# A five-engine schedule of a decoder layer: QK in pairs of banks, a store tile, another down-projection order, new durations and priorities

## The chip, the cores and the metric

One Trainium2 chip, all 8 cores, each with two of the 16 sequences; the cores share no data. The metric is the device time of the slowest core in microseconds (us). These kernels have a second, slower state: the cores of one die (four cores) show a lower granted TensorE clock and the run takes longer (in one run of the changed kernel 0.84 of full speed and 4912.6 us, in a fast one 0.99 and 4295.3 us).

## The reference

One layer of a decoder, d = 1024, sequence 4096, 8 heads of 64, FFN width 2816, with a final norm:

```python
xn = rms_norm(h, mix_norm);  z = xn @ w_in                  # 1024 x 3080
y_conv = gate_b * causal_depthwise_conv(gate_c * u, conv_w)    # 512 wide, 3 taps
# forgetting attention: logit[t, s] = q_t.k_s / 8 + c[t] - c[s], causal, c = cumsum(log f)
y_attn = softmax(logits) @ v                                   # 8 heads x 64
h = h + group_rms_norm(concat(y_conv, y_attn)) @ w_o
gu = rms_norm(h) @ w_gate_up;  h = h + (silu(g) * up) @ w_down   # 2816 wide
h = h + sigmoid(rms_norm(h) @ w_ple_gate + b) * (p @ w_ple_proj)
return rms_norm(h, final_norm)
```

## The kernel before

The kernel works in 16 blocks of 512 tokens a core. It doesn't issue instructions in the order of its source. Each operation is put on record with an engine, a reckoned duration and a priority (`key`; one block is 1.0 wide, smaller is earlier). A scheduler plays the program through on the host, picks on each engine the ready operation with the smallest key, and emits that static order with semaphores. Reckoned durations and keys therefore change only the order and which buffer a tile gets, never the work. On the chip an engine waits at its next instruction: in the trace of the kernel before, VectorE runs nothing from 2314.2 us until an addition that waits for a fetch of h starts at 2321.1.

```python
LAT = {"pe": 0.26, "act": 0.13, "dve": 0.12, "pool": 0.2, "sp": 0.1}
DMA_RATE = 300e3
# ... in Prog.schedule:
                c = clock[e]
                cand = None
                early = None
                for o in lst:
                    r = tile_ready(o)
                    if r is None:
                        continue
                    if r <= c:
                        if cand is None or (o.key, o.seq) < (cand.key, cand.seq):
                            cand = o
                    elif early is None or (r, o.key, o.seq) < early[:3]:
                        early = (r, o.key, o.seq, o)
                if cand is not None:
                    st = (c, cand)
                elif early is not None:
                    st = (early[0], early[3])
                else:
                    continue
                if best is None or st[0] < best[0]:
                    best = st
# ...
            o.start = st
            o.end = st + o.dur
            clock[e] = o.end
```

Attention: each group of four key tiles gets four PSUM banks, four row-tiled QK products (64 of 128 rows, two at once, 4 ns from start to start in the trace; on the diagonal four more for the decay), four exponentials on ScalarE, four PV products. `av` follows `LOOK` units behind.

```python
        LOOK = 4
        # ...
                if ui % 4 == 0:
                    quad = [Tile(qS) for _ in range(4)]

                    def fqk(e, quad=quad, kt=kt, dg=dg, h=h):
                        for dec in ((False, True) if dg else (False,)):
                            for i in range(4):
                                r = slice(64 * (i % 2), 64 * (i % 2) + 64)
                                k_ = ((kt + i) // 2) * 128
                                cc = 128 * i if dg else 0
                                ins = e.matmul(quad[i].ap()[:, cc:T],
                                               lhsT=sel[r, h * 128:(h + 1) * 128] if dec else KT[r, h, k_:k_ + 128],
                                               rhs=crow[r, cc:T] if dec else QT[r, h, cc:T],
                                               start=not dec, stop=dec or not dg)
                        return ins
                    rd = [BKT[h][kt // 4], BQT[h]]
                    if dg:
                        rd += [Bcrow, B["sel"]]
                    last_qk = P.op("pe", fqk, (3 * MM if dg else 2 * MM) + 0.2, K(i), reads=rd, writes=quad,
                                   after=[last_qk])
                st = quad[ui % 4]
                P.op("act", lambda e, st=st, pt=pt, c0=c0, kt=kt, h=h: e.activation(
                    out=pt.ap()[:, c0:T], in_=st.ap()[:, c0:T], func=AF.Exp, bias=bK[:, kt, h:h + 1], scale=1.0),
                    0.17 + (T - c0) / 1200.0, K(i), reads=[st, BbK], writes=[pt])
```

The down projection of each FFN half, the final norm, and the priorities of the main loop (`n` is the block of output projection, FFN, PLE and final norm; PLE is the per-layer embedding, the reference's line with `p`; attention works one block ahead, QKV two):

```python
            for dh in range(2):
                k = L()
                wd = [(wload(g, k), nn) for g, nn in dn[dh]]
                for tt in range(4):
                    k = L()
                    t = Tile(qD)
                    mats = []
                    j = 0
                    for wt, nn in wd:
                        for i in range(nn):
                            mats.append((actT[:, j, tt * 128:(tt + 1) * 128],
                                         (lambda wt=wt, i=i: wt.ap()[:, i * 512:(i + 1) * 512]), [BactT[j], wt]))
                            j += 1
                    mm_group(t, mats, k, [])
                    add_to_h(t, tt, dh, k, scale=0.5)
# ... finish(n, key):
            P.op("dve", lambda e, h=h, c=c: e.scalar_tensor_tensor(out=h[:], in0=h[:], scalar=stat[:, c:c + 1],
                                                                   in1=gfin[:], op0=ALU.mult, op1=ALU.mult),
                 1.25, key, reads=[Bstat[c], B["gfin"]], writes=[Bh[tt]])
            r0 = blk * T + tt * 128
            P.dma("pool", lambda e, h=h, r0=r0: e.dma_start(out=y_d[sq, r0:r0 + 128, :], in_=h[:]), key, f"h{tt}",
                  128 * 4096, reads=[Bh[tt]])
# ... the main loop, b = float(n):
                load_h(n, b - 0.15)
            wo(n, b + 0.0, b + 0.05)
                # ...
                conv(n + 1, b + 0.08, b + 0.5)
                attention(n + 1, b + 0.05, b + 0.8)
            # ...
            ffn(n, b + 0.07, b + 0.68)
            # ...
            ple(n, b + 0.70, b + 0.80)
            finish(n, b + 0.80)
                # ...
                qkv(n + 2, b + 0.5, b + 0.685, b + 0.8, b + 1.055)
```

## Time and profile before

| | before |
|---|---|
| median of the first 4 runs (lowest to highest) | 4422.84 us (4420.14 to 4934.05; the highest is a slow-state run) |
| profiled run: span of the slowest core, its mean granted clock | 4421.6 us, 0.979 |
| TensorE, VectorE, ScalarE busy | 95%, 61%, 53% |

TensorE's busy share is of little use here, since records of successive matmuls overlap (for 512 columns a record lasts 381 ns, the starts lie 216 ns apart). The prediction shows the lines of the profile and splits the span by the distance between the starts of successive matmuls instead (a slot for fewer than 512 columns is taken in proportion: starts lie 163, 109 and 56 ns apart for 384, 256 and 128 columns; what is left over is a mode change, a half-clock slot or a wait).

### The profile page before, as it was taken

How to read it: one execution, taken by the hardware profiler on the slowest of the kernel's cores; microseconds unless marked ns; L12 is line 12 of the kernel's file. 1: busy time of each engine (PE TensorE's matmuls, PEld its weight loads, DVE VectorE, ACT ScalarE, POOL GpSimd, SP SyncE). 2: the span in 40 equal slices, each digit the busy share in tenths (PEclk: the TensorE clock that was granted, in tenths of full speed). 3: DMA queues.
4: the chain of work that ended last, by engine and by line, in shares of the span. 5: the costliest groups of instructions: out<-in, count | busy, mean ns of one | idle time of the engine just before them, and what ended most of it. 6: DMA issues, size and time to landing. Idle time of an engine off the chain costs nothing.

```text
span 4421.6 us, 74502 instructions; the slowest of 8 cores (4402.8 to 4421.6 us)
## 1 busy us (share of the span) xinstructions
PE 4189.6 (95%) x23472; PEld 2006.0 (45%) x23472; DVE 2709.3 (61%) x5508; ACT 2356.9 (53%) x4417; POOL 355.1 (8%) x915
## 2 busy tenths in 40 slices
PE   6898999999999999999989999999999999999987
PEld 3444454454544445444454444545444454444434
DVE  6666676575655656546676766757566565564534
ACT  3333454555656667667234444545566566666721
POOL 2110000000000000001000000000000000000000
PEclk9898999999999999999999999999999999999998
DMA  8796434343433433324444353434334343333232
GB/s 192 168 225 196 134 123 150 129 158 110 139 118 112 160 103 128 116 95 127 143 142 140 117 176 127 155 121 143 119 115 163 109 136 111 106 132 99 93 112 98
DMA packets 172779, 590.32 MB, mean 134 GB/s; under 512 B 19696, under 2 KB 28272, under 8 KB 172400
## 3 DMA queue, kind: packets, MB, share of 16 engines
q1 hardware_dynamic: 127952, 453.80, 30.7%
q0 software_dynamic: 44448, 131.76, 11.8%
q8 instruction: 202, 3.31, 0.3%
q14 instruction: 177, 1.45, 0.1%
HBM read 556.80 MB, written 61.87 MB: 140 GB/s over the span
## 4 chain that ended last, share of the span: by engine, by line
PE 87%; DVE 4%; issue 3%; DMA 3%; ACT 3%; POOL 0%; DVEq 0%; another core or an unknown queue 0%; ACTq 0%; POOLq 0%; SPq 0%
PE ps L577 58%; PE ps L833 11%; PE ps L880 7%; PE ps L1084 5%; PE ps L623 2%; PE ps L701 2%; ACT P L891 1%; DMA xs<-x 1%; DMA y<-h 1%; PE ps L1079 1%; PE ps L863 1%; DMA h<-x 1%; DVE xnTd L628 0%; PE ps L845 0%; DMA wslot<-wscr 0%
## 5 line engine op out<-in xcount | busy, mean ns | idle before, releaser
L891 ACT ACTIVATE P<-ps,bK 128x512 bf16<-128x512 f32 (+3 forms) x2304 | 1364.9, 650 | 747.6 <-PE ps L880 469.4
L577 PE MATMUL ps<-xnTd,wslot 128*128 128x512 bf16 x5792 | 1344.8, 381 | 21.7 <-DVE actT L1030 6.1
L577 PEld LDWEIGHTS ps<-xnTd,wslot 128*128 128x128 bf16 x5792 | 557.4, 98 | 699.4 <-issue 87.8
L833 PE MATMUL ps<-P,VA 128*65 128x512 bf16 (+3 forms) x2304 | 661.3, 368 | 36.5 <-DVE yTa L852 12.7
L577 PE MATMUL ps<-wslot,actT 128*128 128x512 bf16 x2816 | 661.8, 379 | 0.6 <-DVE h L981 0.2
L577 PE MATMUL ps<-xnTq,wslot 128*128 128x512 bf16 x2400 | 571.2, 381 | 8.6 <-DMA wslot<-wscr 4.3
L1026 DVE SCALAR_TENSOR_TENSOR tb<-th,ps 128x512 bf16<-128x512 f32 x352 | 241.2, 685 | 401.1 <-ACT th L1023 382.9
L577 PEld LDWEIGHTS ps<-wslot,actT 128*128 128x128 bf16 x2816 | 271.5, 98 | 322.5 <-issue 19.3
L1023 ACT ACTIVATE th<-ps 128x512 f32<-128x512 f32 x352 | 210.5, 598 | 387.4 <-PE ps L577 385.6
L833 PEld LDWEIGHTS ps<-P,VA 128*65 128x65 bf16 x2304 | 243.5, 111 | 373.1 <-issue 219.1
L981 DVE SCALAR_TENSOR_TENSOR h<-ps,h 128x512 f32<-128x512 f32 x256 | 176.2, 689 | 344.9 <-PE ps L577 323.0
L577 PEld LDWEIGHTS ps<-xnTq,wslot 128*128 128x128 bf16 x2400 | 230.0, 98 | 281.6 <-issue 37.3
L880 PE MATMUL ps<-QT,KT 64*128 64x512 bf16 (+3 forms) x2304 | 338.4, 367 | 12.5 <-ACT P L891 11.7
L895 POOL TENSOR_SCALAR_AFFINE_SELECT P<-P 128x128 bf16<-128x128 bf16 x512 | 180.5, 363 | 1764.8 <-ACT P L891 1674.2
L1030 DVE TENSOR_TENSOR actT<-tb,ps 128x512 bf16<-128x512 bf16 x352 | 240.9, 684 | 121.8 <-PE ps L577 111.3
L607 ACT ACTIVATE xnbf<-h 128x1024 bf16<-128x1024 f32 x196 | 206.3, 1053 | 178.6 <-DVE h L978 88.8
L1084 PE MATMUL ps<-wslot,xnTd 128*128 128x256 bf16 x2048 | 252.3, 278 | 0.0
L1084 PEld LDWEIGHTS ps<-wslot,xnTd 128*128 128x128 bf16 x2048 | 203.8, 100 | 50.8 <-issue 1.6
L909 DVE TENSOR_TENSOR rs<-rs,ps 128x512 f32<-128x512 f32 (+1 forms) x192 | 130.2, 679 | 111.5 <-ACT rs L907 109.3
L623 PE MATMUL ps<-identb,xnbf 128*128 128x128 bf16 x1536 | 125.5, 229 | 62.6 <-DVE xnbf L614 17.7
L628 DVE TENSOR_TENSOR xnTd<-ps,gpc_s 128x1024 bf16<-128x1024 bf16 x132 | 159.0, 1219 | 24.6 <-PE ps L623 23.6
L880 PEld LDWEIGHTS ps<-QT,KT 64*128 64x128 bf16 x2304 | 66.5, 94 | 229.7 <-issue 225.8
(123 smaller groups left out, 4098.0 us busy)
## 6 DMA issues: line engine op xcount, KB each, us to landing
wslot<-wscr SPq DMA_DIRECT2D x795, 512.0 KB, 3.8
h<-x POOLq DMA_DIRECT2D x64, 512.0 KB, 6.0
y<-h POOLq DMA_DIRECT2D x64, 512.0 KB, 7.1
xs<-x POOLq DMA_DIRECT2D x60, 512.0 KB, 4.5
wslot<-wpack POOLq DMA_DIRECT2D x53, 512.0 KB, 14.1
wscr<-wslot SPq DMA_DIRECT2D x53, 512.0 KB, 10.5
wslot<-wscr SPq DMA_DIRECT2D x30, 256.0 KB, 2.8
pbf<-p POOLq DMA_DIRECT2D x16, 256.0 KB, 5.4
```

The costliest lines, as they stand in the source:

```text
L577: ins = e.matmul(out, lhsT=l, rhs=r, start=(i0 + i == 0), stop=(i0 + i == n - 1))
L607: P.op("act", lambda e: e.activation(out=xb.ap()[:], in_=src(), func=AF.Square, accum_out=stat[:, col:col + 1]), 1.25, key - 0.1, reads=[B ...
L623: ins = e.transpose(out=pv[:, kc * 128:(kc + 1) * 128], in_=xb.ap()[:, kc * 128:(kc + 1) * 128], identity=identb[:])
L833: P.op("pe", lambda e, o=o, kt=kt, h=h, pt=pt, c0=c0, first=first, last=last, ui=ui, dg=dg: e.matmul(o.ap()[0:65, c0:T], lhsT=VA[:, kt, h, ...
L880: ins = e.matmul(quad[i].ap()[:, cc:T], lhsT=sel[r, h * 128:(h + 1) * 128] if dec else KT[r, h, k_:k_ + 128], rhs=crow[r, cc:T] if dec els ...
L891: P.op("act", lambda e, st=st, pt=pt, c0=c0, kt=kt, h=h: e.activation(out=pt.ap()[:, c0:T], in_=st.ap()[:, c0:T], func=AF.Exp, bias=bK[:, ...
L895: P.op("pool", lambda e, pt=pt, c0=c0: e.affine_select(out=pt.ap()[:, c0:c0 + 128], in_=pt.ap()[:, c0:c0 + 128], pattern=[[1, 128]], compa ...
L981: P.op("dve", lambda e: e.scalar_tensor_tensor(out=hs, in0=t.ap()[:], scalar=scale, in1=hs, op0=ALU.mult, op1=ALU.add), 0.72, key - 0.05, ...
L1023: P.op("act", lambda e, tg=tg, th=th: e.activation(out=th.ap()[:], in_=tg.ap()[:], func=AF.Tanh, scale=0.5), 0.6, k - 0.1, reads=[tg], wri ...
L1026: P.op("dve", lambda e, tg=tg, th=th, tb=tb: e.scalar_tensor_tensor(out=tb.ap()[:], in0=th.ap()[:], scalar=1.0, in1=tg.ap()[:], op0=ALU.ad ...
L1030: P.op("dve", lambda e, tu=tu, tb=tb, j=j: e.tensor_tensor(out=actT[:, j, :], in0=tb.ap()[:], in1=tu.ap()[:], op=ALU.mult), 0.69, k - 0.1, ...
L1084: ins = e.matmul(tg.ap()[:, i * 256:(i + 1) * 256], lhsT=xnT[1][:, kc, ts], rhs=w8(wg[i])[:, kc, 0:256], start=False, stop=(kc == 7 and i ...
```

## The change

Its intent: a schedule that reckons nearer to the trace (in the trace of before successive 512-column VectorE and ScalarE instructions start 600 and 570 ns apart, though each lasts some 685 ns, on VectorE mostly where the second does not read the first's result, some 790 ns or more where it does; a change between row-tiled and full matmuls costs 96 ns there and 91 ns back), a finer unit for QK, a final norm that frees h at once, an FFN that finishes token tile by token tile, and new priorities. No arithmetic and no byte is added or removed.

```diff
--- before.py
+++ after.py
@@ -60,10 +60,13 @@
 
 class Op:
-                 "npred", "succ", "tag", "lab", "ready", "seq", "start", "end", "vis", "pos", "snap", "waits", "extra")
-
-
-LAT = {"pe": 0.26, "act": 0.13, "dve": 0.12, "pool": 0.2, "sp": 0.1}
+                 "npred", "succ", "tag", "row", "lab", "ready", "seq", "start", "end", "vis", "pos", "snap", "waits", "extra")
+
+
+LAT = {"pe": 0.26, "act": 0.10, "dve": 0.10, "pool": 0.15, "sp": 0.1}
+SELF = {"pe": 0.0, "act": 0.05, "dve": 0.07, "pool": 0.05, "sp": 0.0}
+HEAD = {"pe": 0.0, "act": 0.115, "dve": 0.09, "pool": 0.04, "sp": 0.0}
+SWITCH = 0.1
 DMA_RATE = 300e3
 
 
@@ -170,15 +175,23 @@
                 c = clock[e]
                 cand = None
                 early = None
+                rows = []
                 for o in lst:
                     r = tile_ready(o)
                     if r is None:
                         continue
-                    if r <= c:
+                    if r <= c and o.row:
+                        rows.append(o)
+                    elif r <= c:
                         if cand is None or (o.key, o.seq) < (cand.key, cand.seq):
                             cand = o
                     elif early is None or (r, o.key, o.seq) < early[:3]:
                         early = (r, o.key, o.seq, o)
+                if rows:
+                    o = min(rows, key=lambda o: (o.key, o.seq))
+                    full = sum(1 for f in o.alloc[0].pool.free if f[0] <= c) >= 4
+                    if row_mode or cand is None or (full and (o.key, o.seq) < (cand.key, cand.seq)):
+                        cand = o
                 if cand is not None:
                     st = (c, cand)
                 elif early is not None:
@@ -207,9 +220,12 @@
                 t.pool.free.remove(f)
                 t.idx = f[1]
                 o.extra.extend(f[2])
+            if e == "pe" and o.row != row_mode:
+                st += SWITCH
+                row_mode = o.row
             o.start = st
             o.end = st + o.dur
-            clock[e] = o.end
+            clock[e] = o.end - min(HEAD[e], 0.5 * o.dur)
             if o.sem is not None:
                 t0 = max(o.end + 1.4, dma_free[0])
                 dma_free[0] = t0 + o.nbytes / DMA_RATE
@@ -232,7 +248,7 @@
                     r = 0.0
                     for d in s.deps:
                         if d.eng == s.eng and d.sem is None:
-                            v = d.end if s.eng == "pe" else d.end + 0.065
+                            v = d.end + SELF[s.eng]
                         else:
                             v = d.vis
                         if v > r:
@@ -805,7 +821,7 @@
     def attention(m, k0, k1):
         sq, blk = divmod(m, nblk)
         decay(m, k0 - 0.02)
-        LOOK = 4
+        LOOK = 3
         units = []
         for h in range(8):
             lst = [(kt, 0, False) for kt in range(blk * 4)] + [(blk * 4 + j, 128 * j, True) for j in range(4)]
@@ -868,16 +884,16 @@
                                                                      func=AF.Exp, scale=0.5), 0.6, K(i),
                          reads=[bt], writes=[et])
                 pt = Tile(pP)
-                if ui % 4 == 0:
-                    quad = [Tile(qS) for _ in range(4)]
-
-                    def fqk(e, quad=quad, kt=kt, dg=dg, h=h):
+                if ui % 2 == 0:
+                    pair = [Tile(qS), Tile(qS)]
+
+                    def fqk(e, pair=pair, kt=kt, c0=c0, dg=dg, h=h):
                         for dec in ((False, True) if dg else (False,)):
-                            for i in range(4):
-                                r = slice(64 * (i % 2), 64 * (i % 2) + 64)
-                                k_ = ((kt + i) // 2) * 128
-                                cc = 128 * i if dg else 0
-                                ins = e.matmul(quad[i].ap()[:, cc:T],
+                            for i in range(2):
+                                r = slice(64 * i, 64 * i + 64)
+                                k_ = (kt // 2) * 128
+                                cc = c0 + 128 * i if dg else 0
+                                ins = e.matmul(pair[i].ap()[:, cc:T],
                                                lhsT=sel[r, h * 128:(h + 1) * 128] if dec else KT[r, h, k_:k_ + 128],
                                                rhs=crow[r, cc:T] if dec else QT[r, h, cc:T],
                                                start=not dec, stop=dec or not dg)
@@ -885,17 +901,17 @@
                     rd = [BKT[h][kt // 4], BQT[h]]
                     if dg:
                         rd += [Bcrow, B["sel"]]
-                    last_qk = P.op("pe", fqk, (3 * MM if dg else 2 * MM) + 0.2, K(i), reads=rd, writes=quad,
-                                   after=[last_qk])
-                st = quad[ui % 4]
+                    last_qk = P.op("pe", fqk, MM * (T - c0) / T * (2 if dg else 1) + 0.005, K(i - i % 4), reads=rd,
+                                   writes=pair, after=[last_qk], row=True)
+                st = pair[ui % 2]
                 P.op("act", lambda e, st=st, pt=pt, c0=c0, kt=kt, h=h: e.activation(
                     out=pt.ap()[:, c0:T], in_=st.ap()[:, c0:T], func=AF.Exp, bias=bK[:, kt, h:h + 1], scale=1.0),
-                    0.17 + (T - c0) / 1200.0, K(i), reads=[st, BbK], writes=[pt])
+                    0.26 + (T - c0) / 1200.0, K(i), reads=[st, BbK], writes=[pt])
                 if dg:
                     P.op("pool", lambda e, pt=pt, c0=c0: e.affine_select(
                         out=pt.ap()[:, c0:c0 + 128], in_=pt.ap()[:, c0:c0 + 128], pattern=[[1, 128]],
                         compare_op=ALU.is_ge, fill=zero_reg(e), base=0, channel_multiplier=-1),
-                        0.35, K(i), writes=[pt])
+                        0.29, K(i), writes=[pt])
                 pend.append((h, kt, c0, dg, ui, nu, pt))
             if i >= LOOK:
                 av(i - LOOK)
@@ -1031,22 +1047,27 @@
                                                                          in1=tu.ap()[:], op=ALU.mult),
                      0.69, k - 0.1, reads=[tu, tb], writes=[BactT[j]])
                 done[0] += 16
-            for dh in range(2):
+            last = f_lo > 0
+            if last:
+                wds = [[(wload(g, L()), nn) for g, nn in dn[dh]] for dh in range(2)]
+            for i in range(8):
+                dh, tt = (i % 2, i // 2) if last else (i // 4, i % 4)
                 k = L()
-                wd = [(wload(g, k), nn) for g, nn in dn[dh]]
-                for tt in range(4):
-                    k = L()
-                    t = Tile(qD)
-                    mats = []
-                    j = 0
-                    for wt, nn in wd:
-                        for i in range(nn):
-                            mats.append((actT[:, j, tt * 128:(tt + 1) * 128],
-                                         (lambda wt=wt, i=i: wt.ap()[:, i * 512:(i + 1) * 512]), [BactT[j], wt]))
-                            j += 1
-                    mm_group(t, mats, k, [])
-                    add_to_h(t, tt, dh, k, scale=0.5)
-                    done[0] += f_n
+                if last:
+                    wd = wds[dh]
+                elif tt == 0:
+                    wd = [(wload(g, k), nn) for g, nn in dn[dh]]
+                t = Tile(qD)
+                mats = []
+                j = 0
+                for wt, nn in wd:
+                    for u in range(nn):
+                        mats.append((actT[:, j, tt * 128:(tt + 1) * 128],
+                                     (lambda wt=wt, u=u: wt.ap()[:, u * 512:(u + 1) * 512]), [BactT[j], wt]))
+                        j += 1
+                mm_group(t, mats, k, [])
+                add_to_h(t, tt, dh, k, scale=0.5)
+                done[0] += f_n
 
     def ple(n, k0, k1):
         sq, blk = divmod(n, nblk)
@@ -1106,12 +1127,13 @@
             c = 12 + tt
             sumsq((lambda h=h: h[:]), Bh[tt], c, key, Tile(pXB))
             rsqrt_small(c, 1, key)
-            P.op("dve", lambda e, h=h, c=c: e.scalar_tensor_tensor(out=h[:], in0=h[:], scalar=stat[:, c:c + 1],
-                                                                   in1=gfin[:], op0=ALU.mult, op1=ALU.mult),
-                 1.25, key, reads=[Bstat[c], B["gfin"]], writes=[Bh[tt]])
+            yt = Tile(pX)
+            P.op("dve", lambda e, h=h, c=c, yt=yt: e.scalar_tensor_tensor(
+                out=yt.ap()[:], in0=h[:], scalar=stat[:, c:c + 1], in1=gfin[:], op0=ALU.mult, op1=ALU.mult),
+                 1.25, key, reads=[Bstat[c], B["gfin"], Bh[tt]], writes=[yt])
             r0 = blk * T + tt * 128
-            P.dma("pool", lambda e, h=h, r0=r0: e.dma_start(out=y_d[sq, r0:r0 + 128, :], in_=h[:]), key, f"h{tt}",
-                  128 * 4096, reads=[Bh[tt]])
+            P.dma("pool", lambda e, yt=yt, r0=r0: e.dma_start(out=y_d[sq, r0:r0 + 128, :], in_=yt.ap()[:]), key,
+                  (lambda yt=yt: f"y{yt.idx}"), 128 * 4096, reads=[yt])
 
     for n in range(-2, NB):
         b = float(n)
@@ -1119,30 +1141,30 @@
             load_h(0, -1.6)
         if n >= 0:
             if n:
-                load_h(n, b - 0.15)
+                load_h(n, b - 0.2247)
             wo(n, b + 0.0, b + 0.05)
         if 0 <= n + 1 < NB:
             if n == -1:
                 conv(0, -0.95, -0.6)
                 attention(0, -0.9, -0.3)
             else:
-                conv(n + 1, b + 0.08, b + 0.5)
-                attention(n + 1, b + 0.05, b + 0.8)
+                conv(n + 1, b + 0.0896, b + 0.5446)
+                attention(n + 1, b + -0.0444, b + 0.8)
         if n >= 0:
             for tt in range(4):
                 norm_tile((lambda tt=tt: hT[tt][:]), Bh[tt], tt, 1, 8, 4 + tt, b + 0.05)
-            ffn(n, b + 0.07, b + 0.68)
+            ffn(n, b + 0.1256, b + 0.6909)
             for tt in range(4):
                 norm_tile((lambda tt=tt: hT[tt][:]), Bh[tt], tt, 1, 16, 8 + tt, b + 0.68)
-            ple(n, b + 0.70, b + 0.80)
-            finish(n, b + 0.80)
+            ple(n, b + 0.705, b + 0.7907)
+            finish(n, b + 0.8832)
         if n + 2 < NB:
             if n == -2:
                 qkv(0, -1.4, -1.3, -1.2, -1.1)
             elif n == -1:
                 qkv(1, -0.6, -0.5, -0.4, -0.3)
             else:
-                qkv(n + 2, b + 0.5, b + 0.685, b + 0.8, b + 1.055)
+                qkv(n + 2, b + 0.4402, b + 0.685, b + 0.8495, b + 0.8548)
 
     for o in late:
         if o.key > 0:
```

(`op` takes the `row` flag and `row_mode` starts as False.)

## The prediction

> **What bounds the kernel now.** I read the page's first two parts, then the chain, then TensorE's waits, then two stretches where its share falls. Page of the kernel before (busy us, share of the span, instructions; below them the granted clock in 40 slices):
>
> ```profile
> PE 4189.6 (95%) x23472; PEld 2006.0 (45%) x23472; DVE 2709.3 (61%) x5508; ACT 2356.9 (53%) x4417; POOL 355.1 (8%) x915
> ...
> PEclk9898999999999999999999999999999999999998
> ...
> PE 87%; DVE 4%; issue 3%; DMA 3%; ACT 3%; POOL 0%; DVEq 0%; another core or an unknown queue 0%; ACTq 0%; POOLq 0%; SPq 0%
> ```
>
> TensorE sets the time; VectorE and ScalarE have 39% and 47% to spare. A faster kernel must take away TensorE's waits, not work. Busy time can't tell how much there is, since a matmul's record (381 ns) overlaps its neighbour's. So I took the distance from each matmul's start to the next. For 512 columns the median is 216 ns. Against one such slot per full matmul the 4421.6 us split into: 3785 us full-array work at full clock; 177 us row-tiled QK products (64 rows, two at once, starts 4 ns apart); 109 us of changes between the two modes; 51 us of matmuls at half clock; 27 us of jitter; 242 us of waits (83 us in pieces of 0.1 to 1 us, 159 us in longer ones); 15 us before the first and 15 us after the last matmul.
>
> By region, half clock plus waits over 0.1 us: 63 us up to 200 us (loads), 30 us up to 500, only 29 us from 500 to 1700, 11 up to 2000, 63 us from 2000 to 2600 (end of the first sequence, where attention has few blocks), 34 us from 2600 to 3900, 16 us up to 4195, 33 us in 4195 to 4260, 14 us at the end. The steady part is already dense; what can be had lies at the sequence's joints and in the end.
>
> The two largest single kinds, waits of TensorE (total us, times, longest):
>
> ```profile
> PE ps L577 <- DVE h L978: 24.7, 3, 9.8
> PE ps L623 <- DVE xnbf L614: 17.7, 10, 5.2
> PE ps L623 <- DVE stat L589: 17.4, 2, 15.4
> PE ps L833 <- DVE yTa L852: 12.7, 4, 4.7
> PE ps L880 <- ACT P L891: 11.7, 19, 1.6
> ```
>
> The first is the output projection waiting for the addition to h. The chain between 2300 and 2325 us tells why:
>
> ```profile
> 2304.51 1.29 DVE h L1109
> ...
> 2306.37 8.26 DMA y<-h
> ...
> 2315.22 5.72 DMA h<-x
> ...
> 2321.10 0.70 DVE h L978
> ```
>
> The final norm writes its result over h, the store reads it, and the next block's x may not land in h before the store has landed: 14 us of transfers in series. The next is where attention of the last block runs alone (timeline, 4210 to 4218 us; columns start, length, what, and the idle time before it):
>
> ```profile
> 4210.98 0.61 PE L880 MATMUL ps<-QT,KT 64*128 64x512 bf16 x4 [0.20 <-ACT P L891]
> 4211.68 2.42 ACT L891 ACTIVATE P<-ps,bK 128x512 bf16<-128x512 f32 x4 [0.85 <-PE ps L880]
> ...
> 4214.25 0.61 PE L880 MATMUL ps<-QT,KT 64*128 64x512 bf16 x4 [0.20 <-ACT P L891]
> 4214.95 2.42 ACT L891 ACTIVATE P<-ps,bK 128x512 bf16<-128x512 f32 x4 [0.85 <-PE ps L880]
> ```
>
> A group of four QK products needs all four score banks, so ScalarE stands 0.85 us in each period of 3.27 us.
>
> [...] a full matmul followed by a row-tiled one takes 312 ns start to start, the way back 306 to 308, against 216, so 96 + 91 = 187 ns for a burst; 576 bursts make 108 us. [...] the only granted values are 0.5 and 1, in stretches of 3.41 us or multiples, 188 us in all, nearly each just after a wait; the 10 us wait at 2311 us is followed by 10.24 us at half clock. [...] the 512 KB stores of y took 7.1 us from issue to landing in the median, 2.9 us when the queues were empty at the end.
>
> **The change part by part.** No arithmetic is added or removed: the same matmuls, activations and bytes. It is a new order, and three structural edits.
>
> (1) QK in pairs of banks rather than fours. A row-tiled pair is issued if the last TensorE work was row-tiled, if nothing else is ready, or if all four banks are free and its key is lowest. In dense stages the third rule holds, and the second pair follows the first by the first rule: the 576 bursts stay 576, and 108 us stay. If TensorE would idle, a pair starts at two free banks: up to 0.85 us a group, for about eight groups in the last attention, 7 us. Look-ahead 3 for 4 only moves the PV products a unit earlier.
>
> (2) The final norm writes to one of two xs buffers and the store reads those. The next x can be fetched once the norm has read h: 8.26 us leave the joint. The waits on L978 at 411, 2312 and 2559 us (5.7 + 10.0 + 9.5 = 25 us) and about 10 us of half clock behind them are in reach: 35 us. But four tiles share two buffers: the third norm waits for the first store. The norms now end some 3 to 4 us apart, so the third would start 5 to 6 us after the first has ended, where its store lands 0.6 + 7 to 8 us after: about 3 us of waiting on VectorE, twice a block, 15 blocks: 90 us there, mostly beside TensorE work. I charge 12 us. Net 23 us.
>
> (3) The second half of the down projection runs token tile by token tile. Now all four tiles of h are complete only in the last four groups (2.16 us each), and the four norms follow at 3.4 us each (4372.4, 4375.9, 4379.3, 4382.8 us in the trace). In the new order a tile is complete every 2 x 10 x 0.216 = 4.3 us, so only the last norm, an estimated 6 us, lies bare, in place of 12.6 us: 7 us at the end. At 364 to 377 us (11 us of waits and 6 us of half clock) I take 9, around 2278 us 4: 20 us. In the other blocks attention fills. It holds six of eight weight slots; the next loads (3.8 us to landing) hide behind the norm.
>
> (4) New keys and durations. Attention starts 0.094 of a block earlier, Q is projected 0.2 of a block earlier, the final norm comes later: attention is spread over 0.845 of a block, not 0.75. For the last block this cuts the bare stretch; of its 33 us I take 8 beyond the 7 of (1). Of all other waits and half clock, some 293 in total less 35, 22 and 33 us named above, less the 63 us of the start, some 140 us are open to a better order; I take a quarter, 35 us.
>
> Sum: 7 + 23 + 20 + 8 + 35 = 93 us: 4423 - 93 = 4330 us.
>
> **The rivals.** (a) Pairs split bursts: if half the groups went as two single pairs, 288 more bursts at 187 ns cost 54 us, and the time is about 4384. For it: pairs may start whenever the schedule sees nothing else ready. Against: the first 0.1 us of a change lies then in idle time, and the rule keeps pairs together in dense stages. (b) The two xs buffers become the wait: VectorE stands for stores at each joint. The schedule reckons a store at about 5 us from the norm's end, the trace shows 8 to 9. If a third of the 90 us reached TensorE, 18 us more, about 4348. (c) The keys were searched with a schedule that models VectorE's and ScalarE's overlap better (back-to-back 512-column operations start 600 and 570 ns apart in the trace, though a record lasts 685), so far more than a quarter of the open 140 us goes: two thirds would make about 4270. For it: the four-digit keys look like the result of a search. Against: from 500 to 1700 and 2600 to 3900 us only 63 us are left in 2500, and the start is loads.
>
> **Range and chances.** 2% is 88 us, at 4334: my 93 us stand just across it, so the sides are nearly even. The fixed part (work 3785, QK 177, changes 109, jitter 27, ends 30, start 63) is 4191; even half of the other 230 us, 115, is ambitious. 8 in 10: 4280 to 4385. Faster by over 2%: 0.52; within: 0.46; slower: 0.02, for which rival (a) would have to be more than doubled.
>
> **What would show it.** TensorE's busy time falls little, the span falls. Bursts of QK stay near 576 and ScalarE's wait on L880 in the last attention shrinks. "PE L577 <- DVE h" falls from 25 to under 6 us and no store of y stands ahead of a fetch of h in the chain; VectorE's waits gain a row of the final norm waiting for the store, some 50 to 90 us. The gap before the last block's gate product falls from 12.6 to about 6 us. Half-clock time falls from 188 to about 120 us. Wrong, if mode changes exceed 130 us, if the final norm's wait shows as a wait of TensorE's, or if the region from 500 to 1700 us changes by over 15 us either way.

(The half clock of (2) is in the trace: stretches of 6.8, 10.2 and 10.2 us from 416.0, 2317.2 and 2563.0 us, with 512-column matmuls 427 ns apart. From what the 6 us of (3) are estimated is not on record; 12.6 us less two of the 3.4 us steps between norms would give 5.8. What rival (a) says of a change in idle time can be read from the trace: where TensorE waited for an exponential, the next product starts 144 ns after its end, with a change to row-tiled (19 times) as without one (28 PV products after PV products).)

## The result

Over 17 and 11 runs the medians are 4548.5 us before and 4314.37 us after, but these mix the states: 9 of the 17 runs of before and 4 of the 11 of after were slow. The ratio of the fast runs is 0.9737 (95% interval 0.972 to 0.9755). Ratios here are the mean time of one kernel's fast runs over that of the other's of the same rounds, so not quite the ratio of medians. The lowest runs are 4418.5 and 4294.8 us: 124 us less. (Fast runs of after fall in two groups, near 4295 and near 4312 us; in the second, two neighbouring cores show a clock of 0.984 in place of 0.991. Below I compare lowest runs, which leaves that out.)

The page of after, the same three lines (the slowest core's span is 4293.7 us):

```profile
PE 4164.7 (97%) x23472; PEld 1991.8 (46%) x23472; DVE 2686.3 (63%) x5508; ACT 2340.9 (55%) x4417; POOL 352.2 (8%) x915
...
PEclk9999999999999999999999999999999999999998
...
PE 86%; DVE 6%; issue 4%; DMA 2%; ACT 1%; POOL 0%; DVEq 0%; another core or an unknown queue 0%; ACTq 0%; POOLq 0%
```

The busy time fell by 25 us, the span by 128: the waits went, not the work. The counts of working instructions are the same. TensorE's longest waits after (L593, L639, L849 and L896 are L577, L623, L833 and L880 of before):

```profile
PE ps L639 <- DVE stat L605: 21.0, 3, 16.0
PE ps L639 <- DVE xnbf L630: 15.4, 9, 4.9
...
PE ps L593 <- DVE yTa L868: 4.5, 2, 3.4
PE ps L896 <- ACT P L907: 4.0, 7, 1.2
...
PE ps L593 <- DVE h L994: 0.3, 1, 0.3
```

The 24.7 us for the addition to h are gone (0.3 us), the waits of QK for the exponentials fell from 11.7 to 4.0 us. For the first of these the store tile was hardly needed. The same line without the store tile, in the changed kernel (e7, core 3 of its undisturbed die) and with the new order alone (e13):

```profile
PE ps L593 <- DVE h L994: 2.4, 2, 1.7
```

```profile
PE ps L593 <- DVE h L994: 6.6, 3, 4.9
```

With the store tile alone it is 15.3 us (e2, below). So the new order accounts for most of it. What stays on top in the changed kernel is the first norm at the start (16 us before the first matmul).

The same split by start-to-start distances, of the profiled runs:

| us | before | after |
|---|---|---|
| full-array work + QK products | 3785 + 177 | 3793 + 169 |
| changes of mode (bursts of QK) | 109 (576) | 112 (595) |
| lost to half clock (half-clock time granted) | 51 (188) | 25 (88) |
| waits over 0.1 us | 242 | 127 |
| jitter | 27 | 36 |
| before the first and after the last matmul | 30 | 30 |

So 115 us of waits and 26 us of half clock went. Where: the first addition of the output projection of block 1 comes 26 us earlier than before, that of block 7 67 us, block 10 101 us, block 14 116 us, the last 127 us, and the end comes 128 us earlier. So the start gives 26 us, the first sequence 41, the joint of the sequences (blocks 7 to 10) 34, the second sequence with the last attention 26, the last FFN and the end 1.

The joint, where before a store stood between the norm and the fetch of h. Chain of after, 2235 to 2262 us (start, length, what):

```profile
2238.56 1.20 DVE xs L1131
...
2240.82 10.85 DMA y<-xs
...
2251.77 0.06 DVE xs L1131
...
2252.97 0.69 DVE h L994
```

The store is in this chain still, in another role: the third final norm (L1131) waits for the first store to give back its xs buffer; VectorE idles 3.45 us until 2251.77, and the next addition (L994) starts at 2252.97. No store stands ahead of a fetch of h. VectorE's own wait for it over the whole run is small; view of VectorE's waits of after (total us, times, longest):

```profile
DVE xs L1131 <- DMA y<-xs: 10.8, 6, 3.4
```

The last attention of after (timeline 4085 to 4112 us):

```profile
4090.62 0.60 PE L896 MATMUL ps<-QT,KT 64*128 64x512 bf16 x4
...
4091.11 0.69 ACT L907 ACTIVATE P<-ps,bK 128x512 bf16<-128x512 f32 x1
...
4091.83 1.91 PE L1105 MATMUL ps<-wslot,xnTd 128*128 128x256 bf16 x16
...
4095.63 0.28 PE L896 MATMUL ps<-QT,KT 64*128 64x256 bf16 x2
...
4099.82 2.89 PE L593 MATMUL ps<-wslot,yT 128*128 128x512 bf16 x12
```

PLE matmuls (L1105) lie between the last groups, and 4 us after the last QK product the output projection begins. From the start of the last group of PLE gate products of block 14 to the first addition of the last output projection 46.9 us pass before, 16.3 us after. That is not a gain of 30 us: these gate products end 261 us after the block's output projection has begun before, 281 us after the change.

The end: last addition of the down projection and first gate product before (timeline, 4370 to 4386 us), then the same with the last transposes in after (4244 to 4258 us):

```profile
4371.83 0.68 DVE L981 SCALAR_TENSOR_TENSOR h<-ps,h 128x512 f32<-128x512 f32 x1
...
4384.78 0.58 PE L1079 MATMUL ps<-bple_s,onesrow_s 128*128 128x512 bf16 x1 [1.70 <-DVE xnTd L628]
```

```profile
4247.98 0.69 DVE L997 SCALAR_TENSOR_TENSOR h<-ps,h 128x512 f32<-128x512 f32 x1 [0.25 <-PE ps L593]
...
4250.80 0.61 PE L639 MATMUL ps<-identb,xnbf 128*128 128x128 bf16 x8 [2.92 <-DVE stat L605]
...
4254.33 1.01 PE L639 MATMUL ps<-identb,xnbf 128*128 128x128 bf16 x8 [2.93 <-DVE xnbf L630]
...
4257.03 0.58 PE L1100 MATMUL ps<-bple_s,onesrow_s 128*128 128x512 bf16 x1 [1.70 <-DVE xnTd L644]
```

Two norms, not one, still come after the last matmul: 8.4 us from the end of the last addition to the gate product, 12.3 before (the prediction has 12.6).

### The profile page after: what moved, and what is told of

The parts are those of the page before. It is cut to its first block, busy times and chain, and to the rows that moved or that the text cites. A ratio compares the mean times of both kernels' runs of the same rounds, so it can differ in the third digit from the quotient of the medians.

```text
span 4293.7 us, 74877 instructions; the slowest of 8 cores (4274.2 to 4293.7 us)
## 1 busy us (share of the span) xinstructions
PE 4164.7 (97%) x23472; PEld 1991.8 (46%) x23472; DVE 2686.3 (63%) x5508; ACT 2340.9 (55%) x4417; POOL 352.2 (8%) x915
## 4 chain that ended last, share of the span: by engine, by line
PE 86%; DVE 6%; issue 4%; DMA 2%; ACT 1%; POOL 0%; DVEq 0%; another core or an unknown queue 0%; ACTq 0%; POOLq 0%
PE ps L593 57%; PE ps L849 11%; PE ps L896 7%; PE ps L1105 5%; PE ps L639 2%; PE ps L717 2%; DMA xs<-x 1%; DMA y<-xs 1%; DVE xnTd L644 1%; DVE QT L736 1%; PE ps L1100 1%; PE ps L861 1%; DVE xs L1131 1%; PE ps L879 0%; ACT P L907 0%
## 5 line engine op out<-in xcount | busy, mean ns | idle before, releaser
L593 PE MATMUL ps<-xnTd,wslot 128*128 128x512 bf16 x5792 | 1348.8, 380 | 7.5 <-DVE xnTd L644 3.4
L593 PEld LDWEIGHTS ps<-xnTd,wslot 128*128 128x128 bf16 x5792 | 559.3, 98 | 671.9 <-issue 53.1
L849 PE MATMUL ps<-P,VA 128*65 128x512 bf16 (+3 forms) x2304 | 676.5, 365 | 9.5 <-DVE stat L605 4.8
L593 PE MATMUL ps<-wslot,actT 128*128 128x512 bf16 x2816 | 657.6, 379 | 0.1
L593 PE MATMUL ps<-xnTq,wslot 128*128 128x512 bf16 x2400 | 569.1, 381 | 8.0 <-DVE fst L759 3.5
L593 PEld LDWEIGHTS ps<-wslot,actT 128*128 128x128 bf16 x2816 | 269.6, 98 | 318.9 <-issue 22.7
L849 PEld LDWEIGHTS ps<-P,VA 128*65 128x65 bf16 x2304 | 242.2, 110 | 370.2 <-issue 213.5
L896 PE MATMUL ps<-QT,KT 64*128 64x512 bf16 (+3 forms) x2304 | 360.6, 365 | 4.1 <-ACT P L907 4.0
L593 PEld LDWEIGHTS ps<-xnTq,wslot 128*128 128x128 bf16 x2400 | 231.4, 98 | 268.2 <-issue 27.7
L623 ACT ACTIVATE xnbf<-h 128x1024 bf16<-128x1024 f32 x196 | 207.1, 1057 | 198.3 <-DVE h L994 48.2
L1105 PE MATMUL ps<-wslot,xnTd 128*128 128x256 bf16 x2048 | 247.4, 275 | 0.0
L1105 PEld LDWEIGHTS ps<-wslot,xnTd 128*128 128x128 bf16 x2048 | 201.7, 98 | 47.9 <-issue 1.0
L925 DVE TENSOR_TENSOR rs<-rs,ps 64x512 f32<-64x512 f32 (+1 forms) x192 | 130.1, 678 | 114.6 <-ACT rs L923 109.6
L896 PEld LDWEIGHTS ps<-QT,KT 64*128 64x128 bf16 x2304 | 81.6, 94 | 232.4 <-issue 222.4
L639 PE MATMUL ps<-identb,xnbf 128*128 128x128 bf16 x1536 | 118.5, 223 | 41.9 <-DVE stat L605 21.0
## 6 DMA issues: line engine op xcount, KB each, us to landing
wscr<-wslot SPq DMA_DIRECT2D x53, 512.0 KB, 10.2
```

Of the source, the lines that this page charges most:

```text
L593: ins = e.matmul(out, lhsT=l, rhs=r, start=(i0 + i == 0), stop=(i0 + i == n - 1))
L623: P.op("act", lambda e: e.activation(out=xb.ap()[:], in_=src(), func=AF.Square, accum_out=stat[:, col:col + 1]), 1.25, key - 0.1, reads=[B ...
L639: ins = e.transpose(out=pv[:, kc * 128:(kc + 1) * 128], in_=xb.ap()[:, kc * 128:(kc + 1) * 128], identity=identb[:])
L849: P.op("pe", lambda e, o=o, kt=kt, h=h, pt=pt, c0=c0, first=first, last=last, ui=ui, dg=dg: e.matmul(o.ap()[0:65, c0:T], lhsT=VA[:, kt, h, ...
L896: ins = e.matmul(pair[i].ap()[:, cc:T], lhsT=sel[r, h * 128:(h + 1) * 128] if dec else KT[r, h, k_:k_ + 128], rhs=crow[r, cc:T] if dec els ...
L1105: ins = e.matmul(tg.ap()[:, i * 256:(i + 1) * 256], lhsT=xnT[1][:, kc, ts], rhs=w8(wg[i])[:, kc, 0:256], start=False, stop=(kc == 7 and i ...
```

## The experiments

Each variant carries or leaves out one part of the source; with every part left out the build gives the program of the kernel before, instruction by instruction. Three rounds each; "lowest" is the lowest fast run of the variant against the lowest of the kernel before. The changed kernel itself was run only for the result, not again beside the variants; the lowest runs of the kernel before lie between 4417.3 and 4420.3 us, so a comparison with the changed kernel carries up to 3 us of its own. e1, e3, e9 and e16 had too few fast runs for an interval. All gave correct results. (Expectations of later runs quote gains as ratios of means gave them: 49, 31, 35 and 60 us for e1, e3, e4 and e5, where lowest runs give 45, 28, 29 and 59.) The parts: **durations** (latencies, overlaps, length of an exponential), **priorities** (main loop, look-ahead), **pairs**, **down order**, **store tile**.

Theory 1 is the record: the structure is worth 50 us, the order 43. Theory 2: the order is the main thing, and all parts fill the same holes.

### Each part alone on the kernel before

**e1, durations:**

```diff
-LAT = {"pe": 0.26, "act": 0.13, "dve": 0.12, "pool": 0.2, "sp": 0.1}
+LAT = {"pe": 0.26, "act": 0.10, "dve": 0.10, "pool": 0.15, "sp": 0.1}
-            clock[e] = o.end
+            clock[e] = o.end - min(HEAD[e], 0.5 * o.dur)      # act 0.115, dve 0.09, pool 0.04
-                            v = d.end if s.eng == "pe" else d.end + 0.065
+                            v = d.end + SELF[s.eng]           # act 0.05, dve 0.07, pool 0.05
```

(comments for reading; and 0.26 for 0.17, 0.29 for 0.35 in the exponential and the mask)

> The kernel before with only the durations and latencies of its scheduler replaced (no pairs, old keys, look-ahead 4, norm over h, down projection as before). Theory 1, the one on record (structure: the tile for the store 23 us, the order of the down projection 20, pairs 7; a better order by keys and durations 43 together): at most 20 us, so about 4402 us. Theory 2 (the order itself is the main thing, and the old durations spoiled it by reckoning no overlap between successive VectorE and ScalarE instructions): 50 us or more, below 4372 us, with TensorE's long waits at the joint 2000 to 2600 us shorter although the store still stands ahead of the fetch of h.

Measured: lowest 4372.8 against 4417.8 us, 45 us faster (two fast runs, 4372.8 and 4375.0). Theory 2's 50 us nearly reached, theory 1's 20 exceeded; as theory 2 expected, TensorE's waits and half clock from 2000 to 2600 us fell (from 66 to 45 us in the recount described at e4). No instruction and no transfer was changed, only what the scheduler believes of ScalarE, VectorE and GpSimd.

**e2, store tile:** the diff's part in `finish`.

> The kernel before with only the final norm's result in one of two xs buffers. Theory 1: 23 us faster (35 of waits and half clock less 12 of new VectorE waits), about 4399 us; waits of the output projection on the addition to h fall from 25 to under 6 us. Theory 2: the gap at each joint is filled by other work once the order is good, so alone it brings the same 20 to 35 us, but in the changed kernel nearly nothing. A gain under 10 us speaks against both.

Measured: 4420.3 against 4417.8 us, ratio 0.9994 (0.9932 to 1.0056): nothing, which by the expectation speaks against both theories. The gaps at 2308 and 2552 us shrank from 10.0 and 9.5 to 5.6 and 6.0 us: the fetch of h no longer waits for the store, but it took 10.4 us (issued at 2302.7 us, landed at 2313.1) where it took 5.7 before. That it is slow because of the store is my guess and was not shown: in the trace of before, fetches of h that ran beside a store for over 1 us took 6.1 us in the median (41 of them), the others 5.5 (23). TensorE's waits for the addition fell only to 15.3 us, and VectorE got a new wait; one line of each view of e2:

```profile
PE ps L593 <- DVE h L994: 15.3, 6, 5.9
```

```profile
DVE xs L1131 <- DMA y<-xs: 33.1, 16, 4.5
```

**e3, down order:** the diff's part in `ffn`.

> The kernel before with only the second half of the down projection tile by tile. Theory 1: 20 us faster, about 4402 us, of which 7 us in the gap before the last block's gate products. Theory 2: the four norms after the last matmul are a serial chain of VectorE and ScalarE that is longer than 4.3 us a tile, so the end gains 3 us or less, and the whole under 10 us.

Measured: one fast run, 4390.1 against 4417.8 us, 28 us faster. The profile fell in the slow state; on its undisturbed die the region from 200 to 500 us, where the record expected 9 us, holds 30 us of waits and half clock as before, and 500 to 1700 us fell from 29 to 23. The gap at the end is 8.8 us, 3.5 shorter, where the record expected 7. So size about right, place wrong; theory 2 was nearly right on the end (3 us or less), wrong on the whole.

**e4, pairs:** the diff's parts in `attention` and in the pick of the scheduler.

> The kernel before with only QK in pairs of banks, the rule for row mode and the reckoned cost of a change of mode. Theory 1: 7 us faster, about 4416 us, bursts near 576. Rival a of the record: bursts are split, mode changes over 130 us, slower by 10 us or more. Theory 2: same as theory 1 within 10 us; pairs are not the cause.

Measured: 4388.8 against 4417.8 us, 29 us faster, ratio 0.9921 (0.9873 to 0.9968), four times the expected gain. Counted from the undisturbed die's trace, there are 617 bursts, 64 of them a single pair, and mode changes take 116 us: rival (a) of the record is there in small (7 us) and is outweighed. The number of bursts hides how much the order changed: of the 576 groups of four QK products 244 were split in e4 and 141 in the changed kernel, but their halves often joined a neighbouring group's.

Where the gain lies was recounted on the traces (waits over 0.1 us and half clock; the count runs a little above the record's, which has 29 and 34 us in the first two rows before):

| us | before | e4 | after | e8, after without pairs |
|---|---|---|---|---|
| 500 to 1700 | 36 | 24 | 19 | 34 |
| 2600 to 3900 | 41 | 24 | 29 | 39 |
| 3900 to 4260, with the last attention | 51 | 37 | 37 | 34 |

So on the kernel before pairs help in the dense stretches as well as in the last attention, and in the changed kernel in the dense stretches, not in the last attention, where the record had put all of their worth.

**e5, priorities and look-ahead:** the main loop's lines of the diff, `LOOK = 3`.

> The kernel before with only the priorities of the main loop and the look-ahead of 3. Theory 1 (record): about 8 us from the earlier attention and a part of 35, so 4400 us. Theory 2 (the order is the main thing, each way of ordering better fills the same holes): 40 us or more, 4380 or less.

Measured: 4360.2 against 4419.0 us, 59 us faster, ratio 0.9856 (0.9792 to 0.9921). The largest single part, and the record had put 8 us and a share of 35 on it.

**e6, chance:**

```diff
-MM = 0.2165
+MM = 0.2166
```

> The kernel before with the scheduler's reckoned time of a 512-column matmul moved from 0.2165 to 0.2166 us, which reshuffles the static order and changes nothing else. It measures how much of an effect is chance of the order. Both theories: within 8 us of the kernel before; if it is 20 us or more, effects of single parts of that size say nothing.

Measured: 4415.1 against 4419.0 us, ratio 0.9963 (0.9888 to 1.0037). One sample of chance: 4 us. I take differences under 10 us as not shown.

### Which line, which number

**e16, VectorE's overlap alone** (the edit written out; in the source it is the entry of VectorE in `HEAD`):

```diff
-            clock[e] = o.end
+            clock[e] = o.end - (min(0.09, 0.5 * o.dur) if e == "dve" else 0.0)
```

> The kernel before with one number changed in its scheduler: successive VectorE instructions are reckoned to overlap by 0.09 us. If this is what made the old order wait, 25 us or more of the 49 us of all new durations, 4396 us or less; if it is ScalarE's durations or the latencies, within 12 us of the kernel before.

Measured: one fast run, 4395.7 against 4419.3 us, 24 us faster: half of what all durations give, just short of the expectation's 25.

**e17, the FFN's priorities alone:**

```diff
-            ffn(n, b + 0.07, b + 0.68)
+            ffn(n, b + 0.1256, b + 0.6909)
```

> The kernel before with one line changed: the FFN's priorities run from 0.1256 to 0.6909 of a block in place of 0.07 to 0.68, so attention of the next block goes ahead of it. If the 60 us of the priorities come from the balance of attention against the FFN: 35 us or more, 4386 us or less. If they come from the earlier start of attention, as the record has it: under 15 us.

Measured: 4364.5, 4365.2 and 4365.7 against 4419.3 us: 55 us from one line, nearly all of e5. (The ratio given, 0.9895 with 0.9841 to 0.9948, has a disturbed run in it. Records of some matmuls are missing from this trace, so I don't split its waits.) Attention's start is untouched here; the record's reason, that attention starts 0.094 of a block earlier, is not needed for most of what the priorities are worth. What the line does, counted from the traces over the blocks 1 to 14: the fourth of eight heads is done at 0.525 of the block before and 0.506 in e17, the last FFN gate product comes at 0.646 and 0.653. In the changed kernel it is 0.453 and 0.683. My reading is that the more of attention comes ahead of the FFN, the more full matmuls are left to stand beside what has to wait for ScalarE. That is argued, not tested: the line moves the FFN against the convolution and the next QKV as well.

### Pairs: where the gain is from

**e14, pairs that take all four banks at once (on the kernel before); e15, the same on the changed kernel:**

```diff
-                    full = sum(1 for f in o.alloc[0].pool.free if f[0] <= c) >= 4
+                    full = o.alloc and sum(1 for f in o.alloc[0].pool.free if f[0] <= c) >= 4
...
-                    pair = [Tile(qS), Tile(qS)]
+                    if ui % 4 == 0:
+                        four = [Tile(qS) for _ in range(4)]
+                    pair = four[ui % 4:ui % 4 + 2]
+                    rest = four[2:] if ui % 4 == 0 else ()
...
-                                   writes=pair, after=[last_qk], row=True)
+                                   writes=pair, after=[last_qk], row=True, claim=rest)
```

> The kernel before with pairs, but the first pair of a group takes all four banks, so that none starts at two free banks; the rule for row mode and the reckoned mode change stay. If the 35 us of the pairs alone come from starting at two banks, this is within 8 us of the kernel before (4413 or more). If they come from the finer unit in the order and the rule, it stays near 4386 us. Bursts 576 against 617.

> The changed kernel with the same gating of the first pair. If starting at two banks carries the pairs' gain, about 4320 to 4330 us (as without pairs). If not, 4295 us or some 3 us less, for 19 fewer bursts of 0.19 us.

Measured: e14 4404.1 against 4417.3 us (ratio 0.997, 0.9946 to 0.9994), 13 us faster where full pairs gave 29; e15 4306.1 us, 11 us above the changed kernel. Both have 576 bursts, and no group is split in them. Neither expectation holds alone. Starting at two free banks, and the splitting of groups that comes with it, is worth 16 of the 29 us alone and 11 of the 35 in place. The rest, 13 and 24 us, comes with whole groups, from what e14 and e15 keep: a signal to ScalarE after each pair, the rule of choice, the second pair's priority and the reckoned change of mode. These were not separated. One candidate stands in the traces: where ScalarE waits for a group, the first exponential begins 707 ns after the first QK product before and in e8, 491 ns in e4, e14, e15 and after (in the lines above 4210.98 and 4211.68 us before, 4090.62 and 4091.11 after). On the changed kernel e15 saves 19 bursts (19 x 0.187 = 4 us) and loses more. I expected to see the gain in ScalarE's waits. The exponentials' waits for QK, one line each of before, e8 (after without pairs), after and e15 (total us, times, longest):

```profile
ACT P L891 <- PE ps L880: 469.4, 365, 3.6
```

```profile
ACT P L907 <- PE ps L896: 448.9, 343, 6.3
```

```profile
ACT P L907 <- PE ps L896: 324.9, 277, 6.2
```

```profile
ACT P L910 <- PE ps L899: 378.1, 310, 6.2
```

They fall with pairs, and most where a pair may start at two banks. But this does not make the cause: the exponentials' other wait, for a PV product to give back its buffer, is 163.7 us in e8, 259.8 us after and only 143.7 us in e15, so ScalarE stands less in all in e15, the slower kernel. Through what chain pairs spare TensorE its waits stays open.

### Structure against order

**e12, the three structural parts together; e13, durations, priorities and look-ahead together.**

> The kernel before with the three structural edits together (pairs, down projection tile by tile, tile for the store), old durations, keys and look-ahead. Theory 1 (record): 50 of the whole gain, about 4372 us. Theory 2 (holes are filled by whatever improves the order, so effects overlap): the parts alone gave 35 + 31 + 1 us, together 50 to 65 us, 4360 to 4372 us; what tells the theories apart is the next run.

> The kernel before with only the new durations, keys and look-ahead, no structural edit. Theory 1 (record): 43 us, about 4378 us. Theory 2: durations alone gave 49 us and keys alone about 60, together 80 us or more, below 4342 us; and order plus structure exceed the whole gain of 127 us.

Measured: e12 4347.2 against 4417.3 us, 70 us (three fast runs from 4347 to 4387, ratio 0.9878, 0.9822 to 0.9934); e13 4342.1 us, 75 us (ratio 0.9854, 0.9791 to 0.9916). Theory 1 had 50 and 43. 70 + 75 = 145 us, against 124 for both at once: both sides were too small on record, and 21 us are counted twice. Theory 2 asked for 80 us from the order: nearly.

### Each part taken out of the changed kernel

> The changed kernel with the final norm written over h again. Theory 1: loses 20 us, about 4315 to 4320 us in the undisturbed state. Theory 2: within 10 us of the changed kernel's 4295, since the holes at the joints are filled by attention that starts earlier.

> The changed kernel with QK in groups of four banks again. Theory 1: 7 us slower. Theory 2: pairs gave 35 us alone because they let ScalarE start again before all four banks are free, so 15 to 30 us slower here, about 4315 us, with TensorE's waits for the exponentials back and 576 bursts in place of 595.

> The changed kernel with the down projection as before. Record: 20 us slower, 4315 us. If the parts fill the same holes: 10 us or less slower, about 4305 us, and the gap before the last block's gate products 3 us longer, no more.

> The changed kernel with the old durations and latencies in its scheduler. Alone they gave 49 us. If durations and priorities fill the same holes: 15 to 30 us slower, 4310 to 4325 us. If the durations are a cause of their own: 45 us slower, 4340 us.

> The changed kernel with the old priorities of the main loop (look-ahead 3 kept). If every way of a better order fills the same holes: 10 to 20 us slower, 4305 to 4315 us. If the balance of attention against the FFN is a cause of its own, most of the 60 us are lost: 4340 us or more, and the last stretch of attention alone before the last output projection is again over 30 us.

The edits are those of e1 to e5 the other way round (e11 keeps the look-ahead of 3). In e9 the gap before the last gate product is 11.7 us, 3.3 longer than in the changed kernel, as expected. Its one fast run lies near the record's 4315 us. In e7 the loss lies between the two expectations. In e8 it exceeds both; the 576 bursts are back as expected, TensorE's waits for the exponentials only in small (10.4 us in all, 4.7 in the changed kernel). In e11 the loss is nearer to the second of its expectations (4340 us) than to the first, and in e10 it is below both. Lowest runs; the changed kernel's is 4294.8 us:

| part | alone on before | taken out of after | record |
|---|---|---|---|
| durations | 45 faster | 9 slower (4304.3) | } 8 + 35 |
| priorities | 59 faster | 38 slower (4332.6) | } |
| pairs | 29 faster | 35 slower (4329.6) | 7 |
| down order | 28 faster | 19 slower (4313.6, one run) | 20 |
| store tile | 2 slower | 13 slower (4308.3) | 23 |
| sum | 159 | 114 | 93 |

The column "alone" adds up to more than the whole, the column "taken out" to less: parts fill each other's holes, the durations above all. With the new priorities, the old durations cost under 10 us. The store tile goes the other way: alone it is worth nothing, in a good order 13 us, little above what I take for chance. Priorities and pairs are needed in any case; without either the stretch before the last output projection, counted as above, is longer again (28.4 us without the new priorities, where the expectation was over 30; 32.9 without pairs, 16.3 with both).

### A try at a better version

**e18, the changed kernel with slower transfers reckoned:**

```diff
-                o.vis = dma_free[0] + 0.6
+                o.vis = dma_free[0] + (0.6 if e == "sp" else 2.6)
```

> The changed kernel with the scheduler reckoning 2 us more for each transfer issued by GpSimd. If reckoned transfer times spoil the joints: VectorE's 10.8 us of waits for the store go, and the time falls by 5 to 10 us, to 4287 us. If not: within 5 us of 4295.

Measured: 4301.7 us, ratio to before 0.9731 (0.9703 to 0.9759); against the changed kernel's 4294.8 within chance, though above both expectations. VectorE's wait for the store did fall from 10.8 to 5.0 us, but it bought nothing. No version beat the changed kernel.

## Why the prediction was right or wrong

The side and the range hold: 4330 us with 4280 to 4385 on record, 4295 to 4315 us in fast runs, 2.6% faster where 2.1% was forecast. That the sum came near is in part luck: the terms were off both ways.

- **Step (1), pairs, 7 us: the term was mis-sized.** It measured 29 alone and 35 in place. The step that failed is "In dense stages the third rule holds, and the second pair follows the first by the first rule", with the gain priced only for the last eight groups: 141 of the 576 groups were split (244 in e4), the waits fell in the dense stages, and 13 of the 29 us came with no group split at all (24 of the 35 in place), for which the prediction has no term.
- **Step (2), store tile, 23 us: mis-sized the other way,** 0 alone and 13 in place. "8.26 us leave the joint" failed: the fetch, freed of the wait, took 10.4 us for 5.7 (e2). The wait that it was to end fell from 24.7 to 2.4 us without it in the changed kernel (e7). The charge for VectorE's new wait was also too large: 33 us in e2 and 10.8 in the changed kernel, for the 50 to 90 on record.
- **Step (3), down order, 20 us: size right** (28 and 19), place wrong. The bare chain at the end is 8.4 us, not 6, since the norm of a tile takes longer than the 4.3 us between tiles (5.1 us from the end of the first tile's last addition to its normalised rows, still without the transposes; the third tile's norm also waited 1.8 us until the transposes had freed its buffer), so two are left over; and the hole at 364 us was not filled by it (e3).
- **Step (4), order, 8 + 35 us: the term that failed most.** Alone the order gives 75 us, and one line of it 55 (e17). "I take a quarter" had nothing behind it, and my list of what the keys do (attention and Q earlier, the final norm later) leaves out the FFN's, which e17 shows to carry most of it. Rival (c) named this ("far more than a quarter"), and I argued it down because only 63 us were left in the steady regions. But the change as a whole also took 20 of the 63 us that I had set aside as the loads of the start (43 left), which I had called fixed.
- **Rival (a)** is real and small: 41 more bursts cost 7 us in e4. **Rival (b)**, VectorE standing for stores, is seen in the chain at 2240 us and in e2 (33 us of VectorE's waits); whether it cost e2 its gain is not separated.
- Of the signs named: bursts near 576 (595, though a quarter of the groups were split), L577's wait under 6 us (0.3, but by the order and not by the store tile), no store ahead of a fetch, half-clock time falling (88 us, 120 named), mode changes under 130 us, 500 to 1700 us within 15 us (29 to 16, close to the limit) came true. The end's gap (8.4 for 6) and VectorE's wait (10.8 for 50 to 90) did not.
- **Readings of the prediction that don't hold:** the 10.24 us at half clock at the joint begin at 2317.2 us, inside the wait, which ends at 2321.9; the 22 us among those "named above" in step (4) are named nowhere (step (3) sums to 20). Neither changes a term by more than a few us.

What stays open: through what chain pairs help TensorE (e15), which part of the pairs' edit gives the 13 and 24 us that come with whole groups, what in the FFN's priorities gives the 55 us, why the store tile needs the good order, and how much of each small term is chance; one sample of it, 4 us, is thin.

## What to carry to other kernels

Where a static order is scheduled over several engines and one engine is nearly full, test the balance of two streams by one priority before any restructuring: here a single line gave 55 of 124 us. Don't add up what single edits give; take each out of the final version as well, because edits that fill the same holes look large alone and small together. When a buffer is freed sooner, time the freed transfer again: here it took 10.4 us where it had taken 5.7. And a sign that comes true may do so for another reason: here the wait that the store tile was to end had ended without it.

## What else the traces show

- A change of mode: a full 512-column matmul before a row-tiled one takes 312 ns to the next start, the last row-tiled one before a full one 306 to 308, against 216 without a change: 187 ns a burst, in the changed kernel too (112 us for 595 bursts).
- The granted clock: all eight cores with 95 to 97% busy TensorEs ran whole executions at a mean of 0.978 to 0.983 (the profiled run of before) and 0.990 to 0.994 (that of after); in slow ones the mean of one die's cores was lower (0.839 to 0.845 in one run of the changed kernel, of 4912.6 us).
- Half clock came in stretches of 3.41 us and multiples (188 us in all before, 88 after), 21 of the 22 stretches of before within 4 us of a TensorE wait of 1 us or more, but 9 of 14 after: at 1159.2 us of the changed kernel such a stretch (512-column matmuls start 427 ns apart in it) follows 3.4 us whose only wait was 0.42 us; they held 16 float32 matmuls of 8 to 32 columns.
- Transfers of 512 KB: at the end, with nothing else on the queues, the stores took 2.9 us; amid this kernel stores took 7.1 to 7.3 us and fetches of h 6.0 to 6.4 us in the median. It is the second kind of number that a schedule needs.
- Exponentials of 512 columns last 686 ns and start 570 ns apart: they overlap by 116 ns.
